# Decoder layer on one core: gate/up projection as seven products of half size, its result through DRAM, and the down projection as a stage of its own

## The chip, the core and the metric

One core of a Trainium2 chip runs one launch of the kernel. The metric is the device time of that launch in microseconds, median of the runs; smaller is better. TensorE (PE, with its weight loads as PEld), VectorE (DVE), ScalarE (ACT), GpSimd (POOL) and SyncE (SP, which here only starts transfers) each run their own queue of instructions in order and wait for each other by semaphores.

## The reference

One layer (DEPTH = 1) of a hybrid decoder with D_MODEL = 1024 and D_FF = 2816 on 1024 prompt tokens and 8 sample tokens. Three branches (sparse attention, pooling mixer, memory attention) are merged by gates; the change lies wholly behind that, in the last lines of the layer, with w_gate_up 1024 x 5632 and w_down 2816 x 1024:

```python
def merge_and_ffn(x, l, w, ...):
    ...
    x = x + h @ w['w_out'][l]
    gate, up = jnp.split(rmsnorm(x, w['ffn_norm_g'][l]) @ w['w_gate_up'][l], 2, axis=-1)
    return x + (jax.nn.silu(gate) * up) @ w['w_down'][l]
```

All arrays are fp32.

## The kernel before

**Number format.** Every large product works on fp32r operands in two parts. `split` (L236 to L238) makes them: ACT casts the fp32 source to the high part (L237) and DVE subtracts to get the low part (L238). A product is three matmuls for each 128 of contraction: high with high, high with low, low with high (`mm3` and `gemm`, all matmuls on L255). Tokens lie along the free dimension, T = 1032 of them in `CH`, three chunks of 344, so a matmul is 128x128 weights against 128x344 columns.

**Weights.** `wload` (L240 to L247) brings a 128x1024 tile (512 KB) by a transfer that SP starts into a `wr` buffer, and splits it into `wh` and `wl`. Each of these tags has two buffers.

**Stage A** (up to L1271) computes the three branches and the merge. The change does not touch it.

**Stage B** (L1273 to L1355) has three parts. (1) The output projection: 8 weight tiles of `w_out` against the merged activations `mh`, `ml`, 8 k tiles x 3 chunks x 3 matmuls = 72 matmuls for each weight tile, 576 in all. `ev` (L1291 to L1304) takes each chunk from PSUM: DVE adds the residual `xT` (L1295), the sum `x1` goes to DRAM, ACT scales it into `yh` (L1297), DVE makes `yl` (L1298), ACT squares it (L1303) and POOL adds the squares into `ssq2` (L1304). (2) For each chunk a matmul with ones sums the squares over partitions (L1312), and `rsqrt` (L267 to L276) turns them into 1/rms in `rstd2`: Ln (L272), Exp (L273), then a Newton step; Ln and Exp are in different function tables of ACT, so each pair is recorded with two ACT_TABLE_LOAD. (3) Gate/up and down in four slices of the 22 feature tiles, `SLICES` = 6, 6, 5 and 5 tiles. For each feature tile a gate tile and an up tile of weights run 72 matmuls each; DVE multiplies the chunk by `rstd2` (L1326, L1332), ACT applies Silu (L1327), DVE multiplies the two (L1333), and `split` leaves the product in SBUF as `ah` and `al`. Behind each slice come the 8 weight tiles of `w_dn`, accumulated into `ya`. Gate/up are 44 weight tiles x 72 = 3168 matmuls, down 1584.

**What sets the order.** The tile framework schedules the program with a simulated timeline (`schedule_with_timeline_sim=True`) and so fixes each engine's order of instructions; tile pools with a number of buffers for each tag fix which instruction waits for which release. PSUM has eight banks, tag `g` 1, `s` 3, `t` 3, `p` 1. In stage B, 24 tiles of 128x1032 have the tag `T`, 6 small ones the tag `m`, 5 loading buffers the name `mg`, and 16 tiles the name `XG`, the buffers that hold `mh` and `ml` until the output projection is through.

Of the kernel before, what the change touches and what calls it, by code (L numbers as in the profile page):

```python
# [6 lines left out]
F32 = mybir.dt.float32  # L7
F32R = mybir.dt.float32r
# [38 lines left out]
# attention units at which the gates, then the first part of the merge, start and end  # L47
# [146 lines left out]
def body(nc, tc, xT, memT, w_p, w_m, w_v, w_mk, w_mv, w_up, w_un, w_out, w_gu, w_dn, w_pool, w_cmp, gains, consts, jlt,  # L194
# [83 lines left out]
    # =========================== stage A: projections and the three branches ===========================  # L278
# [35 lines left out]
    # ---- x * g in two exact parts, chunk by chunk; 1/rms per token; the first two projections run along  # L314
# [43 lines left out]
    # ---- a projected tile, rms-normed over groups of partitions  # L358
# [57 lines left out]
    # ---- values and branch gates, tokens on partitions  # L416
# [28 lines left out]
    # ---- memory keys and values of the prompt  # L445
# [7 lines left out]
    # ---- compressed blocks  # L453
# [78 lines left out]
    # ---- merge gates (logits without 1/rms), kept in DRAM until the merge  # L532
# [82 lines left out]
    # ---- pooling mixer  # L615
# [35 lines left out]
    # ---- queries and attention of the memory head by head, between the projections of the pooling mixer  # L651
# [36 lines left out]
    # =========================== the sample group ===========================  # L688
# [8 lines left out]
    # rows of the value pages: partition (page of eight, sixteenth of the page), column (batch, half of its pages)  # L697
# [7 lines left out]
    def pages(src, tab, jobs):  # L705
        """loads of pages: jobs are (destination, place in the page table), 8 places in a row at a time"""
# [29 lines left out]
    # gates, one row per (head, batch)  # L736
# [7 lines left out]
    # scores and pooled blocks, page by page; all rows (head, batch), lower parts in rows 64..127  # L744
# [16 lines left out]
    # window keys: row 0 of the cache has left the window, the new row takes its place  # L761
# [12 lines left out]
    # memory keys  # L774
# [15 lines left out]
    # compressed branch and the choice of blocks  # L790
# [49 lines left out]
    # selected branch: rows 64..127 of Ss carry the second half of the keys  # L840
# [22 lines left out]
    # weights of the pages by half: (token of eight, batch pair, batch of the pair, part, head)  # L863
# [17 lines left out]
    # window weights  # L881
# [14 lines left out]
    # memory weights  # L896
# [17 lines left out]
    # rows (batch of a pair, part, head), columns (batch, feature)  # L914
# [6 lines left out]
    # window values  # L921
# [16 lines left out]
    # memory values  # L938
# [25 lines left out]
    # pages  # L964
# [18 lines left out]
    # the new row and the compressed blocks, then all batches  # L983
# [16 lines left out]
    # ---- prompt attention: compressed, selected (all blocks are selected at this length) and window  # L1000
# [40 lines left out]
    def att_b(u):  # L1041
# [15 lines left out]
        for kt in kts:  # L1057
# [72 lines left out]
    def prep_c(st, kv, i4):  # L1130
        """compressed branch: four heads at once"""
# [40 lines left out]
    # ---- merge of the pooling mixer's and the memory's outputs, which are complete: twice the sum, kept in DRAM  # L1172
# [14 lines left out]
    def gated(mg, wh, wl, n, x, ci, k0, tag):  # L1187
        """(1 + tanh(z / 2)) * (w_up part @ branch output): twice the gated term"""
# [67 lines left out]
    # ---- the attention's part of the merge  # L1256
# [16 lines left out]
    # =========================== stage B: output projection, SwiGLU ===========================  # L1273
    B = ExitStack()
    NT2 = 24
    tp = B.enter_context(tc.tile_pool(name="tB", bufs=NT2))
    sp = B.enter_context(tc.tile_pool(name="sB", bufs=2))

# [3 lines left out]
    def tmp2(w, name):  # L1282
        return sp.tile([128, CW], F32, name=name, tag="m", bufs=NB2)[:, :w]

    yh, yl = [], []
    ssq2 = rstd
    for n in range(8):
        wh, wl = wload(w_out[n], 1024)
        th, tl = T2(F32R, "yh"), T2(F32R, "yl")

        def ev(ci, c0, w, ps):  # L1291
# [17 lines left out]
    rstd2 = rstd
    for c0, w in CH:  # L1310
        ps = psum("s")[:, :w]
        PE.matmul(ps, lhsT=ones, rhs=ssq2[:, c0:c0 + w], start=True, stop=True)  # L1312
        rsqrt(lambda sh, name: tmp2(CW, name="rq"), rstd2[:, c0:c0 + w], ps, w, 1.0 / D)

    ya = [f(XG("ya")) for _ in range(8)]
# [59 lines left out]
```

## Time and profile before

| | |
|---|---|
| device time, median of 3 runs | 1932.1 us (1926.72 to 1936.55) |
| profiled execution, span from the first to the last instruction | 1930.9 us |
| mean granted TensorE clock | 0.986 of full speed |
| PE busy | 96% of the span, 11615 matmul records |
| PEld / DVE / ACT / POOL busy | 92% / 55% / 42% / 24% |
| output projection | about 1082 to 1173 us |
| gate/up and down | about 1173 us to the end |

Busy shares are means over the whole span, and the last 850 us look different from the first 1080, so a change behind 1082 us is read from windows of that stretch. A matmul's recorded duration (about 320 ns for 344 columns) overlaps its neighbours'; what a matmul costs when others follow it is the distance from start to start, which the chain of waits gives as time by count. A row of the chain is a stretch: its start, its length, the engine and line that it was spent on, and how many instructions.

### The profile page before, as it was taken

The numbers are of one execution on the slowest core, as the hardware profiler recorded it, in microseconds if no ns is written. First come the engines' busy times: TensorE is split into PE (matmuls) and PEld (weight loads), VectorE is DVE, ScalarE is ACT, GpSimd is POOL, SyncE is SP. The second block draws the span as 40 slices with busy tenths as digits, with TensorE's granted clock in tenths as the row PEclk, the third lists the DMA queues.
The fourth block names the chain that finished last, engine by engine and source line by source line (L and its number), as shares of the span: only waits on it lengthen the run. The fifth ranks groups of instructions, "written<-read, shape, count | busy, mean of one in ns | idle before, by whom it ended". The sixth has DMA issues, their size and how long they took to land.

```text
span 1930.9 us, 31862 instructions
## 1 busy us (share of the span) xinstructions
PE 1849.5 (96%) x11615; PEld 1783.8 (92%) x11615; DVE 1069.3 (55%) x2469; ACT 814.7 (42%) x1861; POOL 470.6 (24%) x670
## 2 busy tenths in 40 slices
PE   6999997889999999789999999999999999999999
PEld 5998996889888999779988999999999999999999
DVE  7866875652755766788887634333233323333332
ACT  5734774444445776677764435221122112211210
POOL 5300200456243454567754321000000000000000
PEclk9999998999999999989999999999999999999999
DMA  4335128898654111333327542113211111111112
GB/s 163 108 125 161 47 77 132 279 304 287 216 192 147 41 51 66 118 103 94 100 81 220 178 140 81 44 39 94 81 45 42 41 61 44 36 42 66 44 49 94
DMA packets 125551, 209.25 MB, mean 108 GB/s; under 512 B 26217, under 2 KB 89858, under 8 KB 125394
## 3 DMA queue, kind: packets, MB, share of 16 engines
q1 hardware_dynamic: 106210, 166.39, 27.8%
q0 software_dynamic: 7088, 26.02, 4.4%
q10 hardware_dynamic: 12096, 14.80, 2.3%
q8 instruction: 91, 1.49, 0.3%
q14 instruction: 66, 0.54, 0.1%
HBM read 160.46 MB, written 46.70 MB: 107 GB/s over the span
## 4 chain that ended last, share of the span: by engine, by line
PE 61%; DMA 3%; DVE 2%; ACT 2%; issue 1%; POOL 1%; SPq 0%; POOLq 0%; DVEq 0%; ACTq 0%
PE ps_t L255 24%; PE ps_s L255 20%; PE ps_g L255 7%; PE ps_p L1049 3%; PE ps_s L1020 3%; PE ps_t L1065 2%; DMA gt<-gd 1%; DMA wr<-w_up 0%; DMA olr<-od 0%; PE ps_p L255 0%; ACT P L520 0%; POOL P L1039 0%; DVE acc L1266 0%; DVE ptl L238 0%; DMA vpg<-pg_v,ptr 0%
## 5 line engine op out<-in xcount | busy, mean ns | idle before, releaser
L237 ACT CAST wh<-wr 128x512 fp32r<-128x512 f32 (+3 forms) x182 | 146.2, 820 | 365.5 <-PE ps_t L255 166.2
L255 PE MATMUL ps_g<-xh,wh 128*128 128x344 f32 x624 | 205.2, 329 | 5.2 <-ACT mg L541 5.1
L255 PE MATMUL ps_g<-xh,wl 128*128 128x344 f32 x624 | 201.9, 324 | 0.0
L255 PE MATMUL ps_g<-xl,wh 128*128 128x344 f32 x624 | 201.7, 323 | 0.0
L238 DVE TENSOR_TENSOR wl<-wr,wh 128x1024 fp32r<-128x1024 f32 (+3 forms) x156 | 154.3, 995 | 47.9 <-ACT wh L237 46.5
L255 PE MATMUL ps_s<-yh,wl 128*128 128x344 f32 x528 | 169.5, 321 | 0.0
L255 PE MATMUL ps_s<-yh,wh 128*128 128x344 f32 x528 | 169.4, 321 | 0.0
L255 PE MATMUL ps_t<-yh,wl 128*128 128x344 f32 x528 | 169.3, 321 | 0.0
L255 PE MATMUL ps_t<-yh,wh 128*128 128x344 f32 x528 | 169.1, 320 | 0.1
L255 PE MATMUL ps_t<-yl,wh 128*128 128x344 f32 x528 | 168.7, 320 | 0.0
L255 PE MATMUL ps_s<-yl,wh 128*128 128x344 f32 x528 | 168.7, 320 | 0.0
L1039 POOL TENSOR_SCALAR P<-P,st,gate 128x384 f32<-128x384 f32 (+2 forms) x192 | 127.9, 676 | 87.7 <-DVE st L1034 36.9
L1326 DVE TENSOR_TENSOR sg<-ps_s,rstd 128x344 f32<-128x344 f32 x66 | 34.1, 517 | 168.4 <-PE ps_s L255 168.4
L238 DVE TENSOR_TENSOR ptl<-ps_t,pth 128x512 fp32r<-128x512 f32 (+1 forms) x208 | 108.3, 530 | 33.7 <-DMA od<-osb 17.2
L255 PEld LDWEIGHTS ps_g<-xh,wh 128*128 128x128 f32 x624 | 118.1, 189 | 9.1 <-ACT mg L541 7.0
L520 ACT ACTIVATE P<-P,st 128x384 f32<-128x384 f32 (+2 forms) x192 | 112.0, 585 | 29.8 <-DVE st L517 27.4
L255 PEld LDWEIGHTS ps_g<-xl,wh 128*128 128x128 f32 x624 | 118.3, 190 | 2.2 <-issue 0.2
L255 PEld LDWEIGHTS ps_g<-xh,wl 128*128 128x128 f32 x624 | 118.1, 189 | 1.7 <-issue 0.2
L237 ACT CAST pth<-ps_t 128x512 fp32r<-128x512 f32 (+1 forms) x208 | 92.0, 458 | 45.2 <-PE ps_t L1065 31.7
L255 PEld LDWEIGHTS ps_t<-yh,wh 128*128 128x128 f32 x528 | 99.2, 188 | 0.6 <-ACT yh L1297 0.6
L255 PEld LDWEIGHTS ps_s<-yh,wh 128*128 128x128 f32 x528 | 99.2, 188 | 0.1
L255 PEld LDWEIGHTS ps_s<-yh,wl 128*128 128x128 f32 x528 | 99.2, 188 | 0.0
(478 smaller groups left out, 5266.0 us busy)
## 6 DMA issues: line engine op xcount, KB each, us to landing
kpg<-pg_k SPq DMA_DIRECT2D x128, 192.0 KB, 3.9
wr<-w_gu SPq DMA_DIRECT2D x44, 512.0 KB, 3.2
gd<-mg ACTq DMA_DIRECT2D x72, 172.0 KB, 3.6
wr<-w_m POOLq DMA_DIRECT2D x24, 512.0 KB, 5.3
mg<-gd SPq DMA_DIRECT2D x48, 172.0 KB, 2.7
wr<-w_p SPq DMA_DIRECT2D x16, 512.0 KB, 3.6
wr<-w_dn SPq DMA_DIRECT2D x16, 384.0 KB, 3.2
wr<-w_dn SPq DMA_DIRECT2D x16, 320.0 KB, 2.9
```

Source lines behind the costliest of these rows:

```text
L237: (he or S.copy)(hi, src)
L238: (le or V.tensor_sub)(lo, src, f(hi))
L255: PE.matmul(ps, lhsT=x, rhs=y, start=i == 0, stop=i == n - 1)
L520: S.activation(P[u], P[u], AF.Exp, bias=nm, scale=-1.0, accum_out=st[:, 6 + u:7 + u])
L1020: PE.matmul(ps, lhsT=u["q"][:, i * 128:i * 128 + 128], rhs=kk[:, k0 * 128 + a:k0 * 128 + a + n], start=x == 0, stop=x == 1)
L1039: lastp[:] = [G.tensor_scalar(p_, p_, st4[:, j, 5:6], gate[:, q, c:c + 1], op0=ALU.mult, op1=ALU.mult)]
L1049: PE.matmul(pv[:, c0:c0 + n], lhsT=lh, rhs=rhs, start=pvs["n"] == 0, stop=last, skip_group_check=True)
L1065: PE.transpose(pt_[:, x * 128:x * 128 + 128], pd[y][:, o - offs[y]:o - offs[y] + 128], ident)
L1326: V.tensor_mul(s, ps, rstd2[:, c0:c0 + w])
```

## The change

**Output projection.** The chunks are four of 258 tokens (`CH4`; HC = 258, a half HT = 516), and the tiles come in the order 0, 4, 1, 5, 2, 6, 3, 7: 8 x 4 x 24 = 768 matmuls. ACT writes the scaled `x1` as fp32 `y`. As pairs of tiles become complete, `split` writes operands for the halves: B11 (rows 0 to 511 of the contraction, tokens 0 to 515), B21 (rows 512 to 1023, the same tokens), and T2, for which POOL computes `tL` (L1322, L1323). Then `rsqrt` runs over four chunks instead of three.

**Gate/up.** Two weight tiles and the two halves of contraction and tokens make a 2x2 block product, done by Strassen's algorithm in Winograd's form: 7 products of half contraction and half tokens in place of 8. For a pair of weight tiles `wcombos` computes the weight combinations, four POOL operations of 128x512 (L1347, L1349, L1352, L1355), and splits seven operands (7 ACT casts, 7 DVE subtractions). `strassen` runs the seven products, each 2 chunks x 4 k tiles x 3 = 24 matmuls of 258 columns (L1365); 22 calls make 3696. Some products accumulate in PSUM on top of others; the rest is combined by 2 ACT copies (L1380), 14 DVE operations of 128x258 from PSUM and 3 POOL multiplications of 128x516 by `rstd2` (L1394, L1401, L1405). The token operands B22, T1, T3 and T4n are made before the first call, into XG buffers: differences by POOL (L1413, L1417) or DVE (L1421, L1422) through `tL`, which has 2 buffers, then `split`.

**Through DRAM.** Silu and the product of gate and up work on 128x516, and the result goes to a DRAM tensor `acd`.

**Down.** All of gate/up now stands ahead of all of down. Each feature tile comes back from `acd` in three chunks through `mg` buffers and is split; the 1584 matmuls of 344 columns are as before. `NT2` is 20 instead of 24.

```diff
-        gemm(wh, wl, hh_, hl_, KD, ev, "t")
-        yh.append(th)
-        yl.append(tl)
+        gemm(wh, wl, hh_, hl_, KD, ev, "t", CH4)
+        if n < 4:
+            B11[n] = opsplit(T2(F32R, "b11"), yt[:, :HT], HT)
+        else:
+            k = n - 4
+            B21[k] = opsplit(T2(F32R, "b21"), yt[:, :HT], HT)
+            t = sp.tile([128, HT], F32, name="tL", tag="L", bufs=2)
+            G.tensor_sub(t, yt[:, HT:], hn[k][:, HT:])
+            G.tensor_add(t, t, hn[k][:, :HT])
+            T2o[k] = opsplit(T2(F32R, "t2"), t, HT)
...
-    for c0, w in CH:
+    for c0, w in CH4:
         ps = psum("s")[:, :w]
         PE.matmul(ps, lhsT=ones, rhs=ssq2[:, c0:c0 + w], start=True, stop=True)
...
+    def combo(src, w=512):
+        tag = ("wh", "wl", "wx")[cc[0] % 3]
+        cc[0] += 1
+        t = (sp if tag == "wx" else wp).tile([128, 1024], F32R, name="cw", tag=tag, bufs=2)
+        return opsplit(t, src, w)
+
+    def wcombos(s1, s2):
...
+        SY.dma_start(r1, s1)
+        SY.dma_start(r2, s2)
+        a11, a12, a21, a22 = r1[:, :512], r1[:, 512:], r2[:, :512], r2[:, 512:]
...
+        G.tensor_add(x1, a21, a22)
+        r = [combo(a11)]
+        G.tensor_sub(x2, x1, a11)
+        r.append(combo(x2))
+        r.append(combo(a12))
+        G.tensor_sub(x4, a12, x2)
+        r.append(combo(x4))
+        r.append(combo(x1))
+        G.tensor_sub(x3, a11, a21)
+        r.append(combo(x3))
+        r.append(combo(a22))
+        return r
+
+    def product(ps, a, b, first=True):
+        for c in range(2):
+            i = 0
+            for k in range(4):
+                for x, y in ((0, 0), (0, 1), (1, 0)):
+                    PE.matmul(ps[c], lhsT=a[:, x * 512 + k * 128:x * 512 + k * 128 + 128],
+                              rhs=b[k][:, y * HT + c * HC:y * HT + c * HC + HC], start=first and i == 0, stop=i == 11,
+                              skip_group_check=True)
+                    i += 1
...
+    def strassen(w, z1, z2):
...
+        px, py, pq, pr = two("st"), two("st"), two("st"), two("gp")
+        p1, u2 = [], []
+        product(px, w[0], B11)
+        for c in range(2):
+            p1.append(tmp2(HC, "p1"))
+            S.copy(p1[c], px[c])
+        product(py, w[1], T2o)
+        for c in range(2):
+            u2.append(mg(HC))
+            V.tensor_add(u2[c], py[c], p1[c])
+        product(px, w[2], B21, False)
+        for c in range(2):
+            V.tensor_mul(z1[:, q(0, c)], px[c], rstd2[:, q(0, c)])
+        product(pq, w[3], B22)
+        product(pr, w[4], T1)
...
+        G.tensor_mul(z1[:, HT:], z1[:, HT:], rstd2[:, HT:])
+        pz = two("st")
+        product(pz, w[5], T3)
...
+        product(pz, w[6], T4n, False)
...
+    for p in range(NFF // 2):
+        i = 2 * p
+        g1, g2 = T2(name="zg"), T2(name="zg")
+        strassen(w, g1, g2)
+        w = wcombos(w_gu[NFF + i], w_gu[NFF + i + 1])
...
+        u1, u2 = T2(name="zu"), T2(name="zu")
+        strassen(w, u1, u2)
...
+            V.tensor_mul(t[:, c], t[:, c], g[:, c])
+            SY.dma_start(acd[i + j][:, c], t[:, c])
...
+            for c0, n_ in CH:
+                r = mg(n_)
+                SY.dma_start(r, acd[fi][:, c0:c0 + n_])
+                split(r, h[:, c0:c0 + n_], l[:, c0:c0 + n_])
```

The order of ACT before, from the last scaled `x1` of the output projection on (`rq` and `rstd` belong to `rsqrt`):

```order
L1297 ACTIVATE yh<-x_14616,gn 128x344
L272 ACT_TABLE_LOAD
L272 ACTIVATE rq<-ps_s,epst 128x344
L273 ACT_TABLE_LOAD
L273 ACTIVATE rstd<-rq 128x344
L274 ACTIVATE rq<-rstd 128x344
L272 ACT_TABLE_LOAD
```

The order of ACT now at the same place (`t_15011` and `t_15016` are the first two parts of T1, `t_14899` the last of T2):

```order
L1308 ACTIVATE y<-x_14887,gn 128x258
...
L273 ACT_TABLE_LOAD
L273 ACTIVATE rstd<-rq 128x258
L274 ACTIVATE rq<-rstd 128x258
L237 CAST t_15011<-tL 128x516
L272 ACT_TABLE_LOAD
L272 ACTIVATE rq<-ps_s,epst 128x258
L237 CAST t_14899<-tL 128x516
L273 ACT_TABLE_LOAD
L273 ACTIVATE rstd<-rq 128x258
L274 ACTIVATE rq<-rstd 128x258
L237 CAST t_15016<-tL 128x516
```

Casts of token operands, for which matmuls wait, now stand between and behind the table loads; before, nothing but the `rsqrt` itself did.

PE's order now over the first call's fourth and fifth product (`b22` and `t1` are B22 and T1, `cw` weight combinations; x3 stands for the three matmuls of a k tile):

```order
L1365 MATMUL ps_g_15081<-t1_15016,cw_14987 128x258 x2
L1365 MATMUL ps_p_15082<-t1_15016,cw_14987 128x258
L1365 MATMUL ps_s_15075<-b21_14023,cw_14980 128x258 x3
...
L1365 MATMUL ps_t_15076<-b21_14893,cw_14980 128x258 x3
L1365 MATMUL ps_g_15081<-t1_15021,cw_14987 128x258 x3
L1365 MATMUL ps_g_15081<-t1_15026,cw_14987 128x258
```

Work on T1 is cut into single k tiles, with the product on B21 between them. PE's order before in the first gate tile, where the rows go on in this way with no other tile between:

```order
L255 MATMUL ps_s_14675<-yh_13752,wh_14663 128x344
L255 MATMUL ps_s_14675<-yl_13753,wh_14663 128x344
L255 MATMUL ps_s_14675<-yh_13752,wl_14664 128x344
L255 MATMUL ps_s_14675<-yh_13859,wh_14663 128x344
L255 MATMUL ps_s_14675<-yl_13860,wh_14663 128x344
```

PE's order now where the last call ends and down begins (`t4` is T4n, `ah` and `al` the reloaded features):

```order
L1365 MATMUL ps_s_20384<-t4_15070,cw_20230 128x258 x3
L255 MATMUL ps_s_20550<-ah_20460,wh_20546 128x344
L255 MATMUL ps_s_20572<-ah_20460,wh_20546 128x344
L255 MATMUL ps_s_20550<-al_20461,wh_20546 128x344
L255 MATMUL ps_s_20550<-ah_20460,wl_20547 128x344
L1365 MATMUL ps_t_20385<-t4_15052,cw_20230 128x258 x3
```

The first matmuls on reloaded features stand ahead of the last chunk of the last product.

## Rows read from the trace of the kernel before

**Rows 1.** Page: the span, and busy time of each engine

```profile
span 1930.9 us, 31862 instructions
...
PE 1849.5 (96%) x11615; PEld 1783.8 (92%) x11615; DVE 1069.3 (55%) x2469; ACT 814.7 (42%) x1861; POOL 470.6 (24%) x670
```

**Rows 2.** Windows of stage B: us, busy us by engine, clock, DMA share, GB/s

```profile
1082.00:1175.00 93.00, 92.50 (x580) 91.47 (x581) 41.14 (x68) 35.86 (x62) 19.68 (x21) 1.00 0.45 140
1175.00:1313.00 138.00, 137.24 (x866) 136.76 (x866) 52.49 (x90) 41.36 (x63) 0.91 (x1) 1.00 0.14 45
1381.00:1931.00 550.00, 546.52 (x3459) 546.23 (x3457) 193.01 (x320) 96.09 (x151) 0.00 (x0) 1.00 0.16 51
```

**Rows 3.** Waits of PE, 1080 us to the end: total us, times, longest

```profile
PE ps_t L255 <- DVE wl L238: 1.4, 1, 1.4
PE ps_s L1312 <- POOL rstd L1304: 0.8, 1, 0.8
```

**Rows 4.** Chain of waits: start us, length us, engine, tile, line, instructions

```profile
1082.39 90.86 PE ps_t L255 x574
...
1210.67 11.40 PE ps_t L255 x72
```

**Rows 5.** Timeline of PE, matmuls of 280 columns: start us, recorded us

```profile
100.87 0.29 PE L255 MATMUL ps_t<-wvh,xh 128*128 128x280 f32 x1
...
102.28 0.29 PE L255 MATMUL ps_t<-wvh,xl 128*128 128x280 f32 x1
```

**Rows 6.** The same, matmuls of 256 columns

```profile
157.83 0.28 PE L255 MATMUL ps_t<-mh,wh 128*128 128x256 f32 x1
...
160.79 0.28 PE L255 MATMUL ps_t<-ml,wh 128*128 128x256 f32 x1
```

**Rows 7.** Groups by line and form: count, busy us, mean ns, idle before

```profile
L237 ACT CAST wh<-wr 128x512 fp32r<-128x512 f32 x76 | 43.6, 615 | 27.1 <-PE ps_g L255 9.6 <-PE ps_p L255 9.3 <-DMA wr<-w_up 6.7
...
L238 DVE TENSOR_TENSOR wl<-wr,wh 128x512 fp32r<-128x512 f32 x50 | 34.7, 711 | 22.1 <-ACT wh L237 22.1
...
L1326 DVE TENSOR_TENSOR sg<-ps_s,rstd 128x344 f32<-128x344 f32 x66 | 34.1, 517 | 168.4 <-PE ps_s L255 168.4
...
L238 POOL TENSOR_TENSOR wl<-wr,wh 128x512 fp32r<-128x512 f32 x26 | 33.8, 1316 | 16.9 <-ACT wh L237 13.4 <-DVE ptl L238 3.5
...
L1327 ACT ACTIVATE sg<-sg 128x344 f32<-128x344 f32 x66 | 32.3, 489 | 132.5 <-DVE sg L1326 132.5
...
L1304 POOL TENSOR_TENSOR rstd<-rstd,x 128x344 f32<-128x344 f32 x21 | 19.5, 927 | 79.6 <-ACT x L1303 79.6
...
L238 DVE TENSOR_TENSOR ptl<-ps_t,pth 128x256 fp32r<-128x256 f32 x40 | 16.7, 417 | 3.1 <-ACT pth L237 2.4 <-PE ps_p L1049 0.5
...
L237 ACT CAST pth<-ps_t 128x256 fp32r<-128x256 f32 x40 | 14.7, 367 | 13.9 <-PE ps_t L1065 10.3 <-POOL pth L1074 2.7 <-POOL P L1039 0.7
```

**Rows 8.** The same view, 344 columns, SBUF sources only

```profile
L337 DVE SCALAR_TENSOR_TENSOR xl<-xr,gn,xh 128x344 fp32r<-128x344 f32 x24 | 19.9, 864 | 3.8 <-ACT xh L336 3.8
...
L1298 DVE SCALAR_TENSOR_TENSOR yl<-x,gn,yh 128x344 fp32r<-128x344 f32 x24 | 14.2, 590 | 10.5 <-ACT yh L1297 10.5
```

**Rows 9.** Groups by line and form, 1082 us to the end

```profile
L1295 DVE TENSOR_TENSOR x<-ps_t,mg 128x344 f32<-128x344 f32 x24 | 12.4, 516 | 38.7 <-PE ps_t L255 32.4 <-issue 6.3
...
L272 ACT ACT_TABLE_LOAD x3 | 3.8, 1283 | 0.1
L273 ACT ACT_TABLE_LOAD x3 | 3.8, 1283 | 0.1
```

**Rows 10.** A window of stage A

```profile
800.00:850.00 50.00, 34.65 (x196) 31.02 (x196) 41.26 (x95) 31.89 (x78) 28.52 (x37) 0.80 0.44 134
```

**Rows 11.** Waits of PE in that window

```profile
PE ps_t L1161 <- POOL c_s L1158: 9.6, 1, 9.6
```

**Rows 12.** Page: DMA issues, KB each, median us to landing

```profile
wr<-w_gu SPq DMA_DIRECT2D x44, 512.0 KB, 3.2
...
mg<-gd SPq DMA_DIRECT2D x48, 172.0 KB, 2.7
```

More of the change, by code (lines that the diff above doesn't have):

```diff
@@ L1274, in body @@
     B = ExitStack()
-    NT2 = 24
+    NT2 = 20
     tp = B.enter_context(tc.tile_pool(name="tB", bufs=NT2))
     sp = B.enter_context(tc.tile_pool(name="sB", bufs=2))
+    HT = T // 2
+    HC = HT // 2
+    CH4 = tuple((i * HC, HC) for i in range(4))
     def T2(dt=F32, name="t"):
@@ L1282, in tmp2, with opsplit @@
     def tmp2(w, name):
-        return sp.tile([128, CW], F32, name=name, tag="m", bufs=NB2)[:, :w]
-    yh, yl = [], []
+        return sp.tile([128, HC], F32, name=name, tag="m", bufs=NB2)[:, :w]
+    def opsplit(t, src, w):
+        split(src, t[:, :w], t[:, w:2 * w])
+        return t
+    hn = [None] * 8
     ssq2 = rstd
-    for n in range(8):
+    B11, B21, B22, T1, T2o, T3, T4n = ([None] * 4 for _ in range(7))
+    for oi, n in enumerate((0, 4, 1, 5, 2, 6, 3, 7)):
         wh, wl = wload(w_out[n], 1024)
-        th, tl = T2(F32R, "yh"), T2(F32R, "yl")
+        yt = hn[n] = T2(name="y")
         def ev(ci, c0, w, ps):
@@ L1309, in body @@
     rstd2 = rstd
[L1310 removed]
+    for c0, w in CH4:
         ps = psum("s")[:, :w]
         PE.matmul(ps, lhsT=ones, rhs=ssq2[:, c0:c0 + w], start=True, stop=True)
[L1313 to L1315 removed]
+        rsqrt(lambda sh, name: tmp2(HC, name="rq"), rstd2[:, c0:c0 + w], ps, w, 1.0 / D)
+    cc = [0]
+    def combo(src, w=512):
[3 more added lines that the diff above has]
+        return opsplit(t, src, w)
@@ new lines, in product @@
+    def product(ps, a, b, first=True):
[7 more added lines that the diff above has]
+                    i += 1
+    two = lambda t: [psum(x)[:, :HC] for x in t]
@@ new lines, in body @@
+    acd = [dp.tile([128, T], F32, name=f"acd{i}") for i in range(NFF)]
+    w = wcombos(w_gu[0], w_gu[1])
+    for k in range(4):
+        B22[k] = opsplit(XG("b22"), hn[k + 4][:, HT:], HT)
+    for k in range(4):
+        t = sp.tile([128, HT], F32, name="tL", tag="L", bufs=2)
+        G.tensor_sub(t, hn[k][:, HT:], hn[k][:, :HT])
+        T1[k] = opsplit(XG("t1"), t, HT)
+    for k in range(4):
+        t = sp.tile([128, HT], F32, name="tL", tag="L", bufs=2)
+        G.tensor_sub(t, hn[k + 4][:, HT:], hn[k][:, HT:])
+        T3[k] = opsplit(XG("t3"), t, HT)
@@ new lines, in body @@
+    for k in range(4):
+        t = sp.tile([128, HT], F32, name="tL", tag="L", bufs=2)
+        V.tensor_sub(t, hn[k + 4][:, :HT], f(T2o[k][:, :HT]))
+        V.tensor_sub(t, t, f(T2o[k][:, HT:]))
+        T4n[k] = opsplit(XG("t4"), t, HT)
+    for p in range(NFF // 2):
[3 more added lines that the diff above has]
+        w = wcombos(w_gu[NFF + i], w_gu[NFF + i + 1])
+        for t, h in ((g1, 0), (g1, 1), (g2, 1), (g2, 0)):
+            S.activation(t[:, h * HT:h * HT + HT], t[:, h * HT:h * HT + HT], AF.Silu)
+        u1, u2 = T2(name="zu"), T2(name="zu")
+        strassen(w, u1, u2)
+        if p + 1 < NFF // 2:
+            w = wcombos(w_gu[i + 2], w_gu[i + 3])
+        for j, t, g, h in ((0, u1, g1, 0), (0, u1, g1, 1), (1, u2, g2, 1), (1, u2, g2, 0)):
+            c = slice(h * HT, h * HT + HT)
+            V.tensor_mul(t[:, c], t[:, c], g[:, c])
+            SY.dma_start(acd[i + j][:, c], t[:, c])
@@ L1316, in body @@
+    ya = [T2(name="ya") for _ in range(8)]
     for si, (f0, nf) in enumerate(SLICES):
```

44 lines of the change are left out of this document (22 added, 22 removed).

## Prediction

> **What bounds the kernel now.** I read the page first, then windows, then the waits of one engine, then the chain. The page gives a span of 1930.9 us with PE busy 96% of it [rows 1]. That is a mean, so I went to the stretch that the change touches, from 1082 us on: in the windows PE is busy 92.50 of 93, 137.24 of 138 and 546.52 of 550 us, at clock 1.00, while DVE is busy 41.14, 52.49 and 193.01 us and POOL, behind the output projection, does almost nothing [rows 2]. Over the last 850 us PE waits twice, 1.4 and 0.8 us in all [rows 3]. So this stretch is pure matmul time, and what counts is how many matmuls there are, what each costs from start to start, and whether the other engines still keep up. The chain gives the cost: 90.86 us for 574 matmuls of the output projection and 11.40 us for the 72 of a gate tile [rows 4], both 158.3 ns for 344 columns.
>
> **Gate/up matmuls.** Now 3168 x 158.3 ns = 501.5 us. After, 3696 matmuls of 258 columns; none has that width before. The nearest rows are 280 columns, 100.87 to 102.28 us in 11 steps, 128.2 ns [rows 5], and 256 columns, 157.83 to 160.79 us in 25 steps, 118.4 ns [rows 6]. Between 256 and 344 the slope is (158.3 - 118.4)/88 = 0.453 ns a column, so 258 columns cost 118.4 + 0.9 = 119.3 ns and the stage 3696 x 119.3 = 440.9 us: **60.6 us less**. The slope between 280 and 344 (0.470) would give 117.8 ns, 435.4 us. Above, 258 cannot cost more than the 280 row, 128.2 ns, 473.8 us, still 27.7 us less; I take 119.3 because its neighbour is two columns away, and allow 5 us to either side.
>
> The rule that speaks against this change: the Trainium skill, "TensorE: Matmul & The Clock Gate", section "Back-to-back issue gap", gives as sustained spacing 81 ns for 128 columns and 131 ns for 512, so most of a matmul would be a fixed cost. Interpolated (an estimate from that page) this is 98 ns for 258 and 109 ns for 344, and the stage would rise by 3696 x 98 - 3168 x 109 = 17 us. The same section's formula for an isolated pair, columns/2.4 + 2.5 ns, gives 110.0 and 145.8 ns and a saving of 55 us. This case's rows agree with neither figure, but with the second's shape: 118.4 and 158.3 ns are nearly proportional to 256 and 344 columns [rows 4, 6].
>
> **Output projection.** 576 x 158.3 = 91.2 us becomes 768 x 119.3 = 91.6 us: +0.4 us. Its ACT queue gains casts for B11, B21 and T2, but ACT was busy 35.86 of 93 us and POOL 19.68 [rows 2]; that cover holds.
>
> **What a call of the algorithm asks of the other engines.** PE needs 168 x 119.3 = 20.0 us for a call. DVE: seven subtractions of 512 columns at 711 ns, fourteen operations of 258 from PSUM at 417 (the 256 row), and on the mean two multiplications of 516 (711): 5.0 + 5.8 + 1.4 = 12.2 us. ACT: seven casts at 615 ns, two copies at 367, two Silu of 516 taken at the cast's 615 (at 344 columns Silu takes 489 ns): 6.3 us. POOL: four combinations and three multiplications at 1316 ns: 9.2 us; it took 927 ns for 344 columns [rows 7]. Each fits under 20.0 us alone. They are not quite independent: the same kind of DVE operation on 344 columns, two sources in SBUF, takes 864 ns on L337 and 590 on L1298, where POOL works beside it [rows 7, 8], while L1295, with one source in PSUM and in the same stretch as L1298, takes 516 [rows 9], as L1326 does with POOL idle [rows 7]. So I take DVE's two-SBUF work (6.4 us) and POOL's 9.2 us as exclusive: 15.6 of 20.0 us. That fits. In the order, POOL's combinations for the next call stand ahead of the multiplications of the running one, and six operand slots let ACT and DVE prepare them two products ahead; a product is 2.9 us, and the slack of the tightest, the eviction of the sixth product before the next writes that bank, is about that. I put **nothing** on PE in the steady state, and up to 0.5 us a call (11 us) in the range.
>
> The Trainium skill, "SBUF — State Buffer", section "Who interferes with whom", says the same as an exclusive lock: the second of a DVE instruction with two SBUF inputs and a GpSimd instruction that reads SBUF waits for the first. By that rule the rows above agree, and it is the ground of the second rival.
>
> **First transition.** Before, PE ran on through the `rsqrt` at a price of 0.8 us [rows 3], because the first tile needed only `yh`, which was ready. Now T1, T3, T4n and B22 wait for the XG buffers, that is for the last output matmul, and behind it ACT's order has eight table loads of 1283 ns [rows 9] for four Ln/Exp pairs, with the casts of T1 among and behind them. Counted from that matmul: eviction and the scaled copy about 2 us, then four loads (5.1 us), two Ln, two Exp, two squares, two other short operations (about 4 us), so T1's first part is there at about 11 us; two more parts of ACT work of the same kind bring the last at about 23 us. PE has at hand what needs B11, T2's first three parts and B22, some 35 to 45 matmuls (4 to 5 us), before it waits for T1. Behind that POOL has some 14 operations of 516 columns (T1, T3, the next weights), 14 x 1.32 = 18.5 us if alone, nearer 25 with DVE's subtractions against it, and `tL` has two buffers; so the last of T3 comes about 38 us after the last output matmul, by when PE has work for only 25. That is a stall of 13 us, and two more since the clock may fall. Such a fall stands in the trace: in a window of stage A with a PE wait of 9.6 us the clock is 0.80 [rows 10, 11], which is half speed for 20 of 50 us. I take **+15 us**. The ends: 8 if ACT's queue alone decides (23 us against 15 of work), 25 if POOL is stretched throughout and the clock falls for 20 us.
>
> **Second transition.** Down's first slice needs 18 chunks from `acd`. Each transfer takes 2.7 us and a weight tile's 3.2 [rows 12], but only five `mg` buffers exist, of which the last call holds two. Behind a transfer come a cast (0.48) and a subtraction (0.52). So about five chunks come in each 4.5 us, while PE has 2.9 us of matmuls for a k tile of two weight tiles. Ends 1 and 8 us; I take **+4**. Loads hidden under the last call pull towards 1, and its matmuls on T4n, which now stand behind the first on `ah` in PE's order, towards 8. Down itself is unchanged.
>
> **Sum.** 1930.9 - 60.6 + 0.4 - 0.8 (the wait of before) + 15 + 4 = 1888.9 us profiled. The median of the runs is 1.2 us above the profiled span, so **1890 us**.
>
> **Rivals.**
> (a) *POOL and DVE bind the steady state.* If nothing of the two overlaps, a call takes 12.2 + 9.2 = 21.4 us, 1.4 over PE, x 22 = 31 us: about 1921; with a late eviction now and then, up to 1923. For it: [rows 8]. Against it: PSUM-sourced operations are not stretched [rows 9]. Half of it gives 1905.
> (b) *Slower: the queues run in series.* DVE works strictly in order, so a subtraction that waits for ACT's cast, which waits for a POOL combination, holds up the evictions behind it, and PE with them, since only eight banks exist. A call is then POOL 9.2 + DVE 12.2 + the four casts between them 2.5 = 23.9 us, 3.9 x 22 = 86 us: 1976. It decides from (60.6 - 18.6)/22 = 1.9 us a call. Against it: POOL has a whole call of lead in the order.
> (c) *The gain is not there.* The order shows 168 matmuls a call, 3696 in all, so the count is as said. Only a price per matmul that hardly falls with the columns could eat it; break-even is 3168 x 158.3/3696 = 135.7 ns for 258 columns, more than 280 columns take [rows 5]. I give it one chance in a hundred. By the Trainium skill's spacing above (81 and 131 ns) the time would be about 1967 us.
> (d) *A longer first transition*: half clock throughout, 25 to 35 us, gives 1900 to 1910.
>
> **Chances.** Forecast, 1876 to 1904: 0.70. Below that, transitions nearly hidden: 0.05. Half of (a), or (d), 1904 to 1920: 0.12. Full (a), about 1921 to 1930: 0.06. Slower, (b) or (c): 0.07. About 0.5% (9.7 us) is what a measurement of this kernel can tell from no change, so faster means under 1922.4: 0.86, within 0.07, slower 0.07. The range 1876 to 1914 leaves out the ends and holds 0.8.
>
> **What will show it.** The chain of the changed kernel should have stretches of products at 119 ns a matmul, about 20.0 us from call to call, and the waits of PE should lie in the 40 us behind the output projection, released by ACT and DVE for T1 and T3. Waits on DVE in each call would show (a) or (b), with L238 and the POOL lines stretched past 711 and 1316 ns. A granted clock below 1.00 only right behind the first transition is as forecast; later it would make me wrong.

## The result, and the profile after

| | before | after |
|---|---|---|
| device time, median of 4 runs | 1934.3 us | **1901.7 us** (1900.5 to 1903.8) |
| span of the profiled execution | 1930.9 us | 1900.4 us |
| PE busy, matmul records | 1849.5 us, 11615 | 1798.8 us, 12337 |
| DVE / POOL busy | 1069.3 / 470.6 us | 1237.8 / 720.8 us |

The ratio is 0.9842, 95% interval 0.9818 to 0.9865: 1.6% faster. The forecast was 1890, range 1876 to 1914.

The page of the changed kernel, to be set beside [rows 1]:

```profile
span 1900.4 us, 34477 instructions
...
PE 1798.8 (95%) x12337; PEld 1728.6 (91%) x12337; DVE 1237.8 (65%) x2756; ACT 888.5 (47%) x2042; POOL 720.8 (38%) x847
```

Windows of the changed kernel (columns as in [rows 2]): the output projection, three stretches of 20 us behind it, the fourth, then the steady part of gate/up, then down:

```profile
1082.00:1175.00 93.00, 91.32 (x759) 90.91 (x760) 33.95 (x62) 40.70 (x82) 33.54 (x35) 1.00 0.44 133
1175.00:1195.00 20.00, 11.02 (x60) 8.65 (x58) 10.04 (x18) 18.31 (x30) 9.54 (x9) 0.82 0.04 15
1195.00:1215.00 20.00, 18.13 (x130) 16.97 (x129) 16.24 (x23) 13.41 (x23) 13.18 (x10) 0.93 0.09 27
1215.00:1235.00 20.00, 16.15 (x119) 15.73 (x120) 19.96 (x28) 6.47 (x12) 12.26 (x7) 0.91 0.17 57
1235.00:1255.00 20.00, 20.00 (x170) 20.00 (x169) 13.98 (x27) 6.05 (x12) 8.32 (x7) 1.00 0.32 103
1275.00:1640.00 365.00, 365.00 (x3055) 364.71 (x3055) 254.67 (x419) 108.61 (x200) 181.09 (x125) 1.00 0.25 81
1660.00:1901.00 241.00, 235.73 (x1491) 234.70 (x1489) 96.74 (x174) 44.80 (x78) 0.00 (x0) 1.00 0.37 110
```

Read the counts. From 1275 to 1640 us PE ran 3055 matmuls in 365 us without a gap, 119.5 ns each: 168 of them, a call, are 20.07 us. At that pace 20 us hold 167 matmuls; the three stretches behind the output projection hold 60, 130 and 119, so they lack 193, or 23 us, and the granted clock is 0.82, 0.93 and 0.91 there. That is where the time went that was not in the sum. The waits of PE from 1080 us on confirm the place; the first two rows of [rows 3] were all of it before:

```profile
PE ps_g L1365 <- ACT t L237: 5.1, 1, 5.1
PE ps_s L1365 <- DVE t L238: 3.1, 2, 2.8
PE ps_s L1328 <- POOL rstd L1313: 1.6, 2, 0.9
PE ps_t L255 <- DVE wl L238: 1.3, 1, 1.3
PE ps_s L1365 <- DVE u L1399: 1.2, 1, 1.2
PE ps_t L255 <- DVE x L1306: 1.2, 1, 1.2
```

`t` are the parts of T1 and T3 in front of the first call. The long wait, in ACT's timeline (start, length, what; in brackets the idle time before it): four table loads stand between the last scaled `x1` and the first cast of T1.

```profile
1181.56 0.51 ACT L1308 ACTIVATE y<-x,gn 128x258 f32<-128x258 f32 x1
1182.09 1.28 ACT L272 ACT_TABLE_LOAD   x1
...
1184.39 1.28 ACT L273 ACT_TABLE_LOAD   x1
...
1186.43 1.28 ACT L272 ACT_TABLE_LOAD   x1
...
1188.52 1.28 ACT L273 ACT_TABLE_LOAD   x1
...
1190.59 0.61 ACT L237 CAST t<-tL 128x516 fp32r<-128x516 f32 x1
```

The loads are 1283 ns each as in [rows 9], and the cast comes 14.8 us after the last output matmul, which starts at 1175.78 us.

### The profile page after: what moved, and what is told of

Read it like the earlier page. It is cut to its first block, busy times and chain, and to the rows that moved or that the text cites. A ratio compares the mean times of both kernels' runs of the same rounds, so it can differ in the third digit from the quotient of the medians.

```text
span 1900.4 us, 34477 instructions
## 1 busy us (share of the span) xinstructions
PE 1798.8 (95%) x12337; PEld 1728.6 (91%) x12337; DVE 1237.8 (65%) x2756; ACT 888.5 (47%) x2042; POOL 720.8 (38%) x847
## 5 line engine op out<-in xcount | busy, mean ns | idle before, releaser
L255 PE MATMUL ps_g<-xh,wh 128*128 128x344 f32 x624 | 205.3, 329 | 6.3 <-ACT mg L541 6.2
L255 PE MATMUL ps_g<-xh,wl 128*128 128x344 f32 x624 | 201.7, 323 | 0.0
L255 PE MATMUL ps_g<-xl,wh 128*128 128x344 f32 x624 | 201.4, 323 | 0.0
L238 DVE TENSOR_TENSOR wl<-wr,wh 128x512 fp32r<-128x512 f32 (+3 forms) x112 | 100.2, 903 | 56.9 <-ACT wh L237 54.9
L238 DVE TENSOR_TENSOR cw<-tS,cw 128x512 fp32r<-128x512 f32 x88 | 88.5, 1008 | 67.2 <-ACT cw L237 67.1
L255 PEld LDWEIGHTS ps_g<-xh,wh 128*128 128x128 f32 x624 | 117.9, 189 | 10.9 <-ACT mg L541 8.7
L237 ACT CAST cw<-tS 128x512 fp32r<-128x512 f32 x88 | 54.2, 619 | 152.0 <-POOL tS L1349 70.3
L255 PEld LDWEIGHTS ps_g<-xl,wh 128*128 128x128 f32 x624 | 118.1, 189 | 2.0 <-issue 0.2
L255 PEld LDWEIGHTS ps_g<-xh,wl 128*128 128x128 f32 x624 | 117.9, 189 | 1.7 <-issue 0.2
L1365 PE MATMUL ps_t<-b,cw 128*128 128x258 f32 x792 | 111.5, 283 | 2.0 <-ACT b L237 1.1
L1365 PE MATMUL ps_s<-t,cw 128*128 128x258 f32 x792 | 108.3, 283 | 5.0 <-DVE t L238 3.1
L1365 PE MATMUL ps_s<-b,cw 128*128 128x258 f32 x792 | 108.7, 287 | 1.0 <-ACT p L1380 1.0
L1365 PE MATMUL ps_t<-t,cw 128*128 128x258 f32 x792 | 108.1, 283 | 0.3 <-ACT t L237 0.3
L1365 PEld LDWEIGHTS ps_s<-t,cw 128*128 128x128 f32 x792 | 100.4, 190 | 6.3 <-DVE t L238 3.9
L1365 PEld LDWEIGHTS ps_t<-b,cw 128*128 128x128 f32 x792 | 101.9, 189 | 2.7 <-DVE b L238 1.1
L1365 PEld LDWEIGHTS ps_s<-b,cw 128*128 128x128 f32 x792 | 101.9, 194 | 1.5 <-ACT p L1380 1.2
```

What stands on the lines that cost most here:

```text
L237: (he or S.copy)(hi, src)
L238: (le or V.tensor_sub)(lo, src, f(hi))
L255: PE.matmul(ps, lhsT=x, rhs=y, start=i == 0, stop=i == n - 1)
L1365: PE.matmul(ps[c], lhsT=a[:, x * 512 + k * 128:x * 512 + k * 128 + 128], rhs=b[k][:, y * HT + c * HC:y * HT + c * HC + HC], start=first an ...
```

## Experiments

**How the runs are compared.** The stage ahead of the change differs by some microseconds between executions (the first output matmul starts anywhere from 1074 to 1086 us). So the runs are compared by a stretch: from the start of the last output matmul to the start of the last matmul of gate/up, both read from PE's timeline. For the changed kernel these are 1175.8 and 1644.4 us, 468.6 us. Its pure matmul time is 3696 x 119.5 ns = 441.7 us, so 26.9 us are lost. Each row of the table is one profiled execution. How much the stretch scatters between executions was not measured, so differences of 1 or 2 us in it decide nothing alone.

| run | stretch | over pure matmul time | span |
|---|---|---|---|
| changed kernel | 468.6 | 26.9 | 1900.4 |
| one Exp, two table loads | 466.5 | 24.8 | 1894.5 |
| differences on DVE | 467.7 | 26.0 | 1892.9 |
| no operands made | 453.2 | 11.5 | 1885.3 |
| the same and two table loads | 451.0 | 9.3 | 1888.7 |
| operands earlier | 472.9 | 31.2 | 1909.1 |
| operands earlier and three more edits | 457.8 | 16.1 | 1887.4 |
| combinations twice | 509.2 | 67.5 | 1945.7 |
| multiplications twice | 521.9 | 80.2 | 1960.2 |
| six products | 430.6 | 52.0 (pure 378.6) | 1865.7 |
| before, down apart | 504.8 | 3.3 (pure 501.5) | 1928.6 |

**1. Fewer table loads.** In `rsqrt`:

```diff
-        rsqrt(lambda sh, name: tmp2(HC, name="rq"), rstd2[:, c0:c0 + w], ps, w, 1.0 / D)
+        ws.append(tmp2(HC, name="rq"))
+        V.tensor_scalar(ws[-1], ps, -0.5 / D, -0.5 * EPS, op0=ALU.mult, op1=ALU.add)
+        S.activation(rstd2[:, c0:c0 + w], ps, AF.Ln, bias=epst, scale=1.0 / D)
+    S.activation(rstd2, rstd2, AF.Exp, scale=-0.5)
...
```

> One edit to the changed kernel: the four Ln run first and one Exp over all 1032 tokens follows, so two table loads instead of eight. Theory A (ACT's queue decides when the first part of T1 is cast: 14.8 us after the last output matmul, with four table loads of 1.28 us ahead of it): three loads fewer ahead of that cast, so the 5.1 us wait of PE on it goes nearly away, and three fewer behind; PE's waits from 1176 to 1222 us fall by 5 to 8 us, span about 1893 to 1896. Theory B (the two tL buffers and the DVE and POOL operations of their ring decide when the last of T3 and T4n is there, whatever ACT does earlier): the first wait goes but comes back later, gain under 2 us, span 1898 to 1901.

The 5.1 us wait is gone, the largest on ACT is now 1.0 us, but the stretch is only 2.1 us shorter. Waits of PE in this run:

```profile
PE ps_g L1374 <- DVE t L238: 3.3, 3, 2.6
PE ps_s L1374 <- DVE mg L1393: 2.1, 1, 2.1
PE ps_s L1374 <- DVE zg L1396: 1.8, 1, 1.8
```

PE now waits for DVE instead, in the 50 us behind the output projection. The time that a span of 1894.5 seems to add to this comes from the stages before, where the last output matmul starts at 1171.7 us instead of 1175.8. So Theory B is right that the wait comes back later; that the ring of two `tL` buffers is what brings it back is not shown.

**2. Differences on DVE.** `G.tensor_sub` to `V.tensor_sub` for T1 and T3.

> One edit to the changed kernel: the eight differences for T1 and T3 are taken by DVE instead of POOL. Theory B (the ring POOL difference, ACT cast, DVE subtraction through two tL buffers decides, with POOL at 1.3 to 1.7 us for each): a difference takes 0.7 us, the ring turns faster, the waits behind 1205 us (6.8 us in start-to-start gaps) shrink by half, span 1895 to 1898. Theory C (DVE is the narrow engine there, busy 19.96 of 20 us from 1215 to 1235 us): 8 x 0.7 = 5.6 us more on DVE, no gain or up to 4 us lost, span 1900 to 1904.

The stretch is 0.9 us shorter: neither expectation's larger figure came, and the span again owes its gain to an early start (the last output matmul starts at 1169.7 us). Moving this work from POOL to DVE hardly matters here. PE's waits behind the output projection are some 3 us less, but the granted clock of the three 20 us from 1169 us on is 0.83, 0.91 and 0.83, half speed for 17 us instead of 14; which of the two engines holds up which is not shown by this run.

**3. No operands.** This run leaves out B22, T1, T3 and T4n:

```diff
+    B22, T1, T3, T4n = B21, B11, T2o, B21
-    for k in range(4):
-        B22[k] = opsplit(XG("b22"), hn[k + 4][:, HT:], HT)
...
```

> The changed kernel without making B22, T1, T3 and T4n: the products read B21, B11 and T2 in their place (16 casts, 16 subtractions and 16 differences are left out; all matmuls stay). What is left behind the output projection is the eight table loads and the weight combinations. If the operands cause the loss at the first transition (about 25 us over pure matmul time from 1176 to 1262 us), 18 to 22 us go and the span is 1879 to 1882. If the table loads and the rsqrt cause it, less than 10 us go: 1890 or more.

Two of its windows, to be set beside those of the changed kernel, whose clock there was 0.82 and 0.93:

```profile
1175.00:1195.00 20.00, 15.25 (x107) 13.27 (x105) 8.20 (x16) 17.24 (x29) 5.81 (x6) 1.00 0.04 14
1195.00:1215.00 20.00, 18.87 (x155) 18.67 (x156) 14.94 (x30) 9.66 (x19) 9.85 (x7) 1.00 0.23 80
```

Then, with the edit of run 1 too:

> The changed kernel without making B22, T1, T3 and T4n (B21, B11 and T2 are read instead) and with four Ln and one Exp, two table loads instead of eight. Without the operands alone the time from the last output matmul to the end of gate/up was 453.2 us, 11.5 over pure matmul time. If the six table loads (7.7 us of ACT) are what remains: 446 to 449 us. If what remains is the chain of squares, ones matmul and rsqrt on DVE, ACT and POOL: 451 to 454 us.

Without the operands 15.4 of the 26.9 us go, less than the 18 to 22 that would have made them the whole cause; six table loads fewer take away 2.2 more. A part of the 15.4 is the clock: in the changed kernel it stands at half speed for 14 us of the three windows, here it reads 1.00 throughout, and PE's longest wait is 2.1 us instead of 5.1. From PE's timeline, matmuls that start 0.20 to 0.38 us behind the one before without a wait cost about 6 us in the changed kernel and about 1.5 without the operands (an estimate). The last 9.3 us stay without either: in the last run the waits left on PE are for the sum of squares (POOL `rstd`, 2.1 us) and single evictions and copies of 1.2 us or less. No run takes these away, so their cause is only in part known. The largest sum among them:

```profile
PE ps_s L1329 <- POOL rstd L1313: 2.1, 3, 0.9
```

**4. Operands earlier.** The last output tile runs k by k over four PSUM banks, so that `mh` and `ml` come free one after the other, and the operands of three k tiles stand ahead of its evictions:

```diff
-        gemm(wh, wl, hh_, hl_, KD, ev, "t", CH4)
+        if oi < 7:
+            gemm(wh, wl, hh_, hl_, KD, ev, "t", CH4)
+        else:
+            pk = [psum(x)[:, :HC] for x in "stst"]
+            for k in range(KD):
...
+            for k in range(3):
+                operands(k)
+            for ci, (c0, w) in enumerate(CH4):
+                ev(ci, c0, w, pk[ci])
```

> The changed kernel with the last weight tile of the output projection done k by k over four PSUM banks instead of chunk by chunk, so that mh and ml come free one after the other, and with three quarters of B22, T1, T3 and T4n placed ahead of that tile's eviction; table loads and POOL differences stay. Theory O (15 of the 27 us that gate/up takes over its pure matmul time are the operands that wait for XG buffers): the time from the last output matmul to the end of gate/up falls from 468.6 to 455 to 460 us, the span by about 10. Rival (POOL and DVE, which exclude each other, cannot do this work beside the last tile either; it only moves ahead and delays the evictions): 465 us or more.

Slower than the changed kernel, as the rival said. PE's largest wait, and DVE's timeline across it:

```profile
PE ps_t L1393 <- DVE x L1320: 7.2, 1, 7.2
```

```profile
1183.58 1.77 DVE L238 TENSOR_TENSOR t<-tL,t 128x516 fp32r<-128x516 f32 x1
1185.38 0.69 DVE L1308 TENSOR_TENSOR tL<-y,t 128x516 f32<-128x516 f32 x1
1186.11 0.70 DVE L1309 TENSOR_TENSOR tL<-tL,t 128x516 f32<-128x516 f32 x1
1186.72 0.69 DVE L238 TENSOR_TENSOR t<-tL,t 128x516 fp32r<-128x516 f32 x1
1187.33 0.42 DVE L1320 TENSOR_TENSOR x<-ps_s,mg 128x258 f32<-128x258 f32 x1
1187.67 0.42 DVE L1320 TENSOR_TENSOR x<-ps_t,mg 128x258 f32<-128x258 f32 x1
```

The last tile's evictions (L1320) stand in DVE's order behind the operands, and PE needs their banks. With T3's differences on DVE, the table loads of run 1 and the squares written to the loading buffer instead of over `x1`, it looks otherwise:

> The same with three more edits: four Ln and then one Exp (two table loads instead of eight), T3's differences on DVE, and the squares of x1 written to the loading buffer instead of over x1, so that ACT needn't wait for the transfer of x1. If operands and table loads together cause the loss of 27 us: the time from the last output matmul to the end of gate/up is 445 to 452 us and the kernel takes 1879 to 1886 us. If a part of the loss is inherent in the sum of squares and rsqrt that everything waits for (11 us were left without the operands): 453 to 458 us, 1887 to 1892 us.

1889.1 us (1888.1 to 1890.7), ratio to before 0.9786, interval 0.9762 to 0.9810: **the fastest kernel of the study** among those that leave nothing out, since its interval ends below where that of the changed kernel begins (0.9818). The stretch is 457.8 us, so the second of the two expectations held by its number; that the rest is inherent in the sum of squares is not shown. The three edits were not run apart, so which of them made the early operands pay stays open. Its windows:

```profile
1174.00:1194.00 20.00, 15.40 (x101) 12.80 (x100) 18.77 (x29) 16.93 (x33) 10.50 (x9) 0.99 0.16 53
1194.00:1214.00 20.00, 17.30 (x126) 16.50 (x127) 18.76 (x33) 9.26 (x18) 9.70 (x7) 0.84 0.15 50
1214.00:1234.00 20.00, 20.00 (x170) 20.00 (x169) 15.86 (x26) 5.54 (x10) 10.79 (x8) 1.00 0.20 71
```

PE reaches its pace 40 us behind the last output matmul instead of 59; until then DVE is busy 18.8 of 20 us.

**5. How much room a call has.** Each of the four combinations is done twice on POOL:

```diff
         G.tensor_add(x1, a21, a22)
+        G.tensor_add(x1, a21, a22)
```

> The changed kernel with each of the four weight combinations on POOL done twice (the second writes the same values): POOL goes from about 10.3 to 16 us of the 20.05 us of a call. Theory A (PE alone sets the pace of a call; the stretch of DVE and POOL is hidden): a call stays at 20.05 us and the span moves by at most 4 us, at the first transition. Rival (POOL and DVE, which exclude each other, have little left): DVE's operations with two SBUF sources, about 10 us a call when stretched, no longer fit beside 16 us; a call becomes 22 us or more and the span rises by 40 us or more.

The rival's number came. A call went from 20.07 to 22.2 us (2266 matmuls, 13.5 calls, in 300 us). The waits of PE, then windows of the steady part of this run and of the changed kernel:

```profile
PE ps_s L1369 <- DVE u L1403: 24.9, 12, 3.1
```

```profile
1300.00:1600.00 300.00, 282.48 (x2266) 280.73 (x2265) 198.99 (x313) 78.76 (x147) 217.39 (x151) 0.96 0.22 71
```

```profile
1300.00:1600.00 300.00, 300.00 (x2511) 299.71 (x2510) 210.35 (x344) 90.65 (x166) 153.40 (x105) 1.00 0.24 79
```

No engine is full: POOL is busy 217 of 300 us, DVE 199. Against 2266 matmuls at full pace the 300 us lose 29 us. Eight of the twelve waits lie in them, 17.5 us; the granted clock of 0.96, half speed for 24 us, can hold up to 12 more. So the longer call is waits and, behind them, a slower PE. One of the twelve waits, on POOL, ACT, DVE and PE in that order:

```profile
1480.59 1.40 POOL L1347 TENSOR_TENSOR tS<-wr 128x512 f32<-128x512 f32 x1 [4.87 <-DMA wr<-w_gu]
```

```profile
1486.12 0.62 ACT L237 CAST cw<-tS 128x512 fp32r<-128x512 f32 x1 [6.02 <-POOL tS L1351]
```

```profile
1486.78 1.22 DVE L238 TENSOR_TENSOR cw<-tS,cw 128x512 fp32r<-128x512 f32 x1 [5.01 <-ACT cw L237]
...
1488.70 0.42 DVE L1403 TENSOR_TENSOR u<-ps_s,mg 128x258 f32<-128x258 f32 x1
```

```profile
1489.18 2.09 PE L1369 MATMUL ps_s<-t,cw 128*128 128x258 f32 x8 [2.58 <-DVE u L1403]
```

POOL waited for the weight tile, then ran the doubled chain; ACT waited for POOL, DVE's subtraction for ACT, and the evictions behind it in DVE's order (L1403 among them) for that subtraction; PE waited 2.58 us for the bank. DVE stood still for 5.01 us here.

To see whether the place of POOL's work matters, the same load went to the multiplications by 1/rms, into unused buffers:

> The changed kernel with four more POOL operations in each call, as in the run with doubled combinations, but at another place: they repeat the multiplications by 1/rms (128x516, into unused tL buffers). POOL's load grows by the same 5.2 to 6 us a call. Theory L (the sum of POOL's and DVE's two-SBUF work, which exclude each other, sets the pace then): the loss is the same as with doubled combinations, 35 to 45 us. Theory H (there the loss came from DVE's order: a subtraction that waits for ACT's cast of a POOL combination stands ahead of PSUM evictions; the combinations come late because POOL starts them when the weight tile has landed): the multiplications stand ahead of Silu and of the product of gate and up only, so at most 15 us are lost.

```profile
PE ps_s L1365 <- DVE u L1401: 33.5, 11, 3.6
```

```profile
1300.00:1600.00 300.00, 275.67 (x2180) 274.24 (x2180) 207.45 (x298) 79.17 (x145) 211.06 (x146) 0.94 0.20 69
```

The stretch loses 53 us against the changed kernel, where the doubled combinations lose 41. So the claim of Theory H that this place is nearly free falls, and the 35 to 45 us of Theory L are missed too. Part of the difference is the clock, 0.94 here, half speed for 36 of 300 us. The result doesn't prove Theory L: POOL works in order too, so late multiplications make the next combinations late, and DVE in this run still waits mostly for casts, the mechanism of Theory H, as its waits from 1300 to 1600 us show (in the changed kernel this row is 54.5 us, the longest 4.2, and PE waits for nothing):

```profile
DVE cw L238 <- ACT cw L237: 60.3, 26, 5.1
```

What is shown is that a call of 20 us has no room for 5 to 6 us more on POOL at either of the two places tried; how much of that is the exclusion and how much the order of the queues stays open.

Then the other way, PE's work cut: the run leaves out the seventh product's matmuls.

```diff
-        product(pz, w[6], T4n, False)
```

> The changed kernel without the seventh product of each call (the one on T4n; its operands are still made, all evictions stay): 3168 matmuls instead of 3696, a call is 144 x 119.5 ns = 17.2 us of PE work while DVE, ACT and POOL keep theirs. Theory A (PE alone sets the pace): 22 x 24 x 119.5 ns = 63 us less, span about 1837. Theory L (DVE's two-SBUF work, 6.4 us, and POOL's, 9.2 us unstretched, exclude each other, 15.6 us in series, and the order lets little of the rest be idle): with 17.2 us a call evictions come late, PE waits 0.5 to 1.5 us a call on DVE, span 1848 to 1870.

The stretch fell by 38.0 of 63.1 us, and the span of 1865.7 us is within Theory L's range. From 1300 to 1600 us, with 144 matmuls a call, the window and PE's largest wait:

```profile
1300.00:1600.00 300.00, 283.69 (x2321) 278.57 (x2322) 197.91 (x372) 94.17 (x178) 164.99 (x113) 1.00 0.27 85
```

```profile
PE ps_s L1365 <- ACT p L1380: 12.1, 8, 1.5
```

2321/144 = 16.1 calls in 300 us, 18.6 us a call instead of 17.2. The size is as Theory L said, but PE does not wait where it said, on DVE: of 16.3 us of waits 13.5 are for ACT's copy `p`. In ACT's order this copy stands behind a Silu that waits for POOL (in the instance at 1483.42 us, for 2.80 us). So with six products a call takes about 18.6 us in this order, held up by the chain from POOL through ACT. If the same floor holds with seven products, the changed kernel hides it under PE's 20.07 us with 1.5 us to spare; that is an estimate, since PE's own products are links of the chain and the seventh gives it time.

**6. Down apart, alone.** The kernel before with its features through DRAM and down behind all of gate/up:

```diff
-                split(u, th[:, c0:c0 + w], tl[:, c0:c0 + w])
+                SY.dma_start(acd[fi][:, c0:c0 + w], u)
...
+            for c0, n_ in CH:
+                r = mg(n_)
+                SY.dma_start(r, acd[fi][:, c0:c0 + n_])
+                split(r, h[:, c0:c0 + n_], l[:, c0:c0 + n_])
```

> The kernel before with one part of the change alone: gate/up (3168 matmuls of 344 columns as before) all ahead of down, the features through DRAM, split again after loading. If the way through DRAM is hidden but for the start of down (1 to 2 us in the changed kernel, where down takes 252.2 us against 250.8 us of matmuls): span 1931 to 1935. If the 132 more transfers or the second pass of casts disturb the weight tiles: 1940 or more.

From the last output matmul to the last matmul of the kernel 755.2 us, against 754.3 before: this part costs 0.9 us, or nothing that can be told from it.

## Why the prediction held, and where it was off

**Bound and count: right.** Gate/up's gain is the matmul count times the narrower pace. 119.3 ns were put down from the row for 256 columns [rows 6]; 119.5 were measured, 0.7 us on the stage. The Trainium skill, "TensorE: Matmul & The Clock Gate", section "Back-to-back issue gap", has 81 ns for 128 and 131 ns for 512 columns as sustained spacing, by which this change would have lost. The trace differs: 119.5 ns at 258 and 158.3 at 344.

**Steady state: right in its result, with less room than reckoned.** PE waits nowhere from 1275 to 1640 us. But DVE's part is 254.67 us in 18.2 calls, 14.0 us a call instead of 12.2, because the two-SBUF subtractions are stretched while the operations from PSUM are not (groups of the steady part, 1300 to 1600 us, to be set beside [rows 7]):

```profile
L238 DVE TENSOR_TENSOR cw<-tS,cw 128x512 fp32r<-128x512 f32 x60 | 60.4, 1007 | 50.8 <-ACT cw L237 50.6
L238 DVE TENSOR_TENSOR cw<-wr,cw 128x512 fp32r<-128x512 f32 x45 | 52.9, 1176 | 4.0 <-ACT cw L237 3.9
...
L1355 POOL TENSOR_TENSOR tS<-wr 128x512 f32<-128x512 f32 x15 | 26.2, 1746 | 0.0
...
L1347 POOL TENSOR_TENSOR tS<-wr 128x512 f32<-128x512 f32 x15 | 19.8, 1321 | 72.9 <-DMA wr<-w_gu 72.9
...
L1384 DVE TENSOR_TENSOR mg<-ps_t,p 128x258 f32<-128x258 f32 x15 | 6.3, 422 | 6.4 <-PE ps_t L1365 6.4
```

1007 and 1176 ns stand against 711 before, 1746 against 1316 on POOL (L1355; of the other combinations L1347 stays at 1321 ns, L1352 at 1295, and L1349 takes 1445), and 422 against 417 from PSUM. That fits the exclusive lock of the Trainium skill, "SBUF — State Buffer", section "Who interferes with whom". This lock is the ground of rival (a). The slow rival (b) named the right mechanism, queues in series: run 5 shows it step by step once POOL is given 5 us more. It doesn't decide here by about 1.5 us a call. "A whole call of lead in the order", held against it, was wrong: POOL starts the combinations when the weight tile lands, and waits for it, 72.9 us in 15 calls (L1347), so the lead is much shorter than the order suggests. The tile lands late because the tag `wr` has two buffers and a pair of weight tiles takes both: SyncE can start the next transfer only when DVE's last subtraction from the old tile is done, as its waits of the same 300 us show:

```profile
SPq L1342 <- DVE cw L238: 103.1, 15, 9.8
```

So POOL waits for DVE through the buffers, too. No run gives `wr` more buffers, and what that would be worth is not known. That the steady state cost nothing was therefore in part luck: the reason given against (b) did not hold, and the margin was small.

**First transition: the term that was mis-sized.** 15 us were put down, with 25 as the far end; the stretch lost 26.9. Of the steps, T1's first cast was put at 11 us behind the last output matmul and came at 14.8: the last scaled `x1` alone came at 5.8 (1181.56 us), where 2 had been taken. The last of T3 was put at 38 us. POOL's last difference nearly kept to that, it ended at 1216.15 us, 40 us behind; but its low part was begun only at 1219.54 us and done 44 us behind, since DVE had become the full engine, 19.96 of 20 us busy from 1215 us on, with weight combinations and T4n in the same order. The sum had followed ACT's queue and POOL's, and DVE's only as what stretches POOL. The clock, taken as 2 us, reads 0.82, 0.93 and 0.91: half speed for 36%, 14% and 18% of the three windows, 14 us in all, which cost about 6 us (the estimate of run 3). The runs show that no single step of it was the cause: without the operands 15.4 us go, some 5 of them by the clock, and with fewer table loads 2. The 9 us that stay are in part waits for the sum of squares, which the sum had not counted apart; the rest is not traced to a cause. In size the result is nearest to rival (d), 25 to 35 us there and 1900 to 1910 us, but the half clock that (d) blamed is about a quarter of it. The loss lies above the far end that the term itself was given. That the total stayed within the range is owed to the room that the range had for other terms, above all the steady state, which took none of it.

**Output projection: +0.4 forecast, +2.8 measured** (from first to last matmul 95.3 us instead of 92.5). The row L255 <- DVE x L1306 among the waits, 1.2 us, is a part of it.

**Second transition: +4 forecast, +1.4 measured.** From the last matmul of gate/up to the last of the kernel 252.2 us, against 1584 x 158.3 ns = 250.8. (Four of these matmuls run ahead of the last product, so 0.6 us more belongs here and not to the first transition.) Loads from `acd` run under the last call, which was the case at the low end.

**Sum.** First transition 11.9 us more than put down, output projection 2.4 and pace 0.7 more, second transition 2.6 less; and before, the same place had cost 2.0 us (754.3 against 752.3 us of matmuls) where the 0.8 of one wait was taken off, 1.2 less. That is 11.2 of the 11.5 us between 1888.9 and the span of 1900.4.

## What to carry to other kernels

An algorithm that saves matmuls pays in full only while the other engines' chain for one unit of work fits under PE's time for it; measure that room by cutting PE's work or doubling another engine's, since busy shares (here 70% and 51%) don't show it. A change of operands in the middle of a pipeline costs a refill: list everything that must happen between the last reader of the old buffers and the first use of the new ones, on every queue, and look for work that PE can do meanwhile. When one wait is taken away there and the time stays, the next queue in the chain has taken its place, and several edits may be needed together (run alone, three of them gave 2.1, 0.9 and -4.3 us; with a fourth, and the second in part, 10.8 us, where the fourth was never run alone).

## What was not expected of the hardware

DVE's subtraction of 128x512 or 128x516 from two SBUF sources takes 0.68 us or up to 1.79 us, and POOL's operation of that size 1.29 or 1.75 us, in the same stretch (run 4's timeline shows 0.69 and 1.77 in neighbouring rows): not a slow-down of both by a share, but a wait of one for the other. The changed kernel shows it closely. Two pairs from its timeline, a DVE subtraction begun while POOL worked and one begun just before:

```profile
1495.73 1.30 POOL L1352 TENSOR_TENSOR tS<-wr,tS 128x512 f32<-128x512 f32 x1
...
1496.34 1.24 DVE L238 TENSOR_TENSOR cw<-tS,cw 128x512 fp32r<-128x512 f32 x1 [3.77 <-ACT cw L237]
...
1500.80 0.68 DVE L238 TENSOR_TENSOR cw<-tS,cw 128x512 fp32r<-128x512 f32 x1
...
1500.96 1.68 POOL L1394 TENSOR_TENSOR zg<-zg,rstd 128x516 f32<-128x516 f32 x1 [2.23 <-DVE zg L1393]
```

In the first, DVE ends at 1497.58 us, 0.55 behind POOL's end; in the second DVE keeps its 0.68 us and POOL takes 1.68 instead of 1.30. From 1300 to 1600 us all 53 subtractions that began during a POOL operation ended 0.546 to 0.556 us behind that operation's end, whether they took 1.14 or 1.79 us, and all that began before one or with POOL idle took 0.68 to 0.69.
